# Deeper weight prefetch in the second output projection, and the first FFN matrix's second token group with contraction pairs outermost

## The chip, the cores and the metric

The kernel runs on one core of one Trainium2 chip. The metric is device time in microseconds (us) of one execution; the time of a version is the median over its runs. TensorE does matmuls and transposes (PE in the rows; PEld is its weight load), VectorE (DVE) and ScalarE (ACT) do elementwise work, GpSimd (POOL) and SyncE (SP) here mostly issue transfers.

## The reference

One step of a hybrid decoder layer in fp32, for 1024 prompt tokens and 8 sample tokens, model width 1024:

```python
mp, ... = mixer_prompt(yp * (1 + scp) + shp, w_in, sinks, gn_w, w_out)   # attention + retention, ends in [..] @ w_out
yp = layer_norm(ALPHA * yp + (1 + gtp) * mp, ln1_w, ln1_b)
g, u = split(( yp * (1 + scp2) + shp2 ) @ w_up, 2)                         # D_FF = 2816
yp = layer_norm(ALPHA * yp + (1 + gtp2) * ((silu(g) * u) @ w_down), ln2_w, ln2_b)
```

The same is done for the sample tokens. The change touches the place where the output projection (`@ w_out`) of the second half of the tokens ends, the first layer norm runs, and the first of the `w_up` matrices starts.

## The kernel before, in words

**Exactness.** Every fp32 operand of a large matmul is split into a high part (an ACT copy into a shortened format) and a low part (a DVE subtraction). A product is three matmuls, `mm3` (lines 215 to 217): high x high, high x low, low x high. So TensorE can run only when ACT and DVE have both parts of both operands.

**Output projection.** `out_proj(half, with_s)` works on 512 tokens: two column groups (`cg`) of 512 columns, four units (`kp`) of 256 contraction rows each. A unit's weights are loaded as one 512 KB tile `raw` (line 256, on SP's queue), `w_hi` makes `wh` (line 269, ACT), `w_lo` makes `wl` (line 281, DVE). `w_get` is called for each unit and runs these three ahead by the three numbers of `depth`: loads, high parts, low parts. It starts as `[2, 1, 0]`, and the second half sets it. The rows of `x` for the residual (`xr`, line 1152, and `xrs` for the samples) are loaded at the fourth unit of the first column group. In the second column group of the second half, tile 0 runs through all four units first and tiles 1 to 3 follow; `out_evac` (lines 1117, 1118) multiplies by the gate and adds the residual, and `ln1_tile` normalizes a tile (DVE statistics, a power on POOL, line 1238 on ACT). `poutz` (line 1174) is the samples' product.

**Input of the FFN.** `h2_group(g)` builds the right-hand side for token group g (512 tokens; group 1 also carries the samples, so its tiles have 260 columns instead of 256). For each of four contraction pairs j, `blocks(j)` transposes two 128-row slices through PSUM (`h2p`, line 1292) and scales them into `ht` (line 1293, ACT). Of `ht` come `hb` (split of two quarters, lines 1305 and 1306), `ts` (three differences, lines 1318 to 1320), `hs` (split of `ts` by the helper `split`, lines 1351 and 1352) and `hc` (split of one quarter, lines 1324 and 1325).

**FFN matrices.** Each matrix i is multiplied by a scheme with seven products (`STEP`, p = 1, 2, 6, 7, 5, 3, 4) instead of eight. Products 1 and 2 read `hb`, 3 reads `hc`, and 4 to 7 read `hs`. `up(i, gs)` has the product outermost, then the group, then the pair j; products that are only summed share a PSUM bank, and `up_out` evacuates them. The weights are prepared by `up_prep`: `up_load` (`wr`, line 1361), `up_sums` (lines 1370 to 1373) and the splits `wa`, `wb`, `wc` (lines 1351, 1352) and `wd` (1392, 1393), some steps ahead; for matrices after the first only once `"ahead"` is in `done`. `up_prep(-7)` and `up_prep(-3)` for the first matrix stand between the tiles of the projection's last column group.

**Order.** The generators emit work in an interleaving that `Merge` makes from the nanoseconds in each `yield`; `("need", x)` waits until x is in `done`. A main stream (`out_proj`, then `ffn`) runs with side streams (`ln1_tile`, `h2_group`, ...) at a ratio (1.73 and 1.9). The tile framework then orders each engine's instructions, with earlier emission as priority, and gives out buffers: 46 pages of 1040 columns for nearly everything in SBUF, 8 banks in PSUM. A page is given back when its last reader is done, and a load may have to wait for one.

In `ffn`, the first matrix is done for group 0, then for group 1, then all other matrices for both groups.

Of the kernel before, what the change touches and what calls it, by code (L numbers as in the profile page):

```python
# [12 lines left out]
AF = mybir.ActivationFunctionType  # L13
ALU = mybir.AluOpType
# [10 lines left out]
WID = 256, 260  # L25
# [152 lines left out]
def emit(ctx, tc, I, O):  # L178
# [10 lines left out]
    def bank(name, dt=F32):  # L189
        return psp.tile([128, 512], dt, name=name, tag="ps", bufs=8)  # L190
# [7 lines left out]
    def f(ap):  # L198
        return ap.bitcast(F32)

    M = Merge()
    done = M.done
# [925 lines left out]
    def out_proj(half, with_s):  # L1128
        yield ("need", ("att", half))
        if half == 1:  # L1130
            depth[:] = [3, 2, 1]
        for cg in range(2):
            by_tile = half == 1 and cg == 1
            ps = [bank(f"pout{t}") for t in range(4)]
# [141 lines left out]
    def h2_group(g):  # L1276


        n = WID[g]
        for t in range(4):  # L1280
            yield "need", ("xn", 4 * g + t)
        yield "need", "ab2"
        if g:
            yield "need", "xns"
        def blocks(j):
            ht = page(f"ht{g}_{j}")
            hv = ht[:, 0:4 * n].rearrange("p (s b c) -> p s b c", s=2, b=2)
            for s in range(2):
                kt = 2 * j + s
                b = bank("h2p")  # L1290
                for i in range(4):
                    PE.transpose(b[:, i * 128:(i + 1) * 128], xr[4 * g + i][:, kt * 128:(kt + 1) * 128], ident)
                A.activation(out=hv[:, s, :, 0:256], in_=b.rearrange("p (b c) -> p b c", b=2), func=AF.Identity,
                             scale=A2[:, kt, 0:1], bias=B2[:, kt, 0:1])
                if g:
                    V.tensor_copy(out=hv[:, s, :, 256:260], in_=h2ts[:, kt, :].rearrange("p (b c) -> p b c", b=2))
            return ht

        hts = []
        for j in range(4):  # L1300
            ht = blocks(j)
            hts.append(ht)
            h3 = ht[:, 0:4 * n].rearrange("p (q c) -> p q c", q=4)
            hb = page(f"hb{g}_{j}", F32R)
            A.copy(out=hb[:, 0:2 * n].rearrange("p (q c) -> p q c", q=2), in_=h3[:, 0::2, :])  # L1305
            V.tensor_sub(out=hb[:, 2 * n:4 * n].rearrange("p (q c) -> p q c", q=2), in0=h3[:, 0::2, :],  # L1306
                         in1=f(hb[:, 0:2 * n]).rearrange("p (q c) -> p q c", q=2))
            HB[g, j] = hb
            yield 880, 0, 1000
        for t in range(4 * g, 4 * g + 4):  # L1310
            x = xr.pop(t)
            G.dma_start(out=yd[t], in_=x[:, 0:1024])
        done.add(("h2b", g))
        for j in range(4):
            ht, hts[j] = hts[j], None
            h3 = ht[:, 0:4 * n].rearrange("p (q c) -> p q c", q=4)
            ts = page(f"ts{g}_{j}")
            V.tensor_sub(out=ts[:, 0:2 * n].rearrange("p (q c) -> p q c", q=2), in0=h3[:, 1::2, :], in1=h3[:, 0:2, :])
            V.tensor_sub(out=ts[:, 2 * n:3 * n], in0=h3[:, 3], in1=ts[:, 0:n])
            V.tensor_sub(out=ts[:, 3 * n:4 * n], in0=h3[:, 2], in1=ts[:, 2 * n:3 * n])  # L1320
            if j % 2 == 0:
                hc = page(f"hc{g}_{j}", F32R)
            HC[g, j], o = hc, 2 * n * (j % 2)
            A.copy(out=hc[:, o:o + n], in_=h3[:, 3])
            V.tensor_sub(out=hc[:, o + n:o + 2 * n], in0=h3[:, 3], in1=f(hc[:, o:o + n]))
            HS[g, j] = split(ts, f"hs{g}_{j}", 4 * n)
            yield 0, 0, 3400
        done.add(("h2", g))
        yield 0, 0

# [18 lines left out]
    def split(t, name, n=1024):  # L1349
        h, l = page(name + "h", F32R), page(name + "l", F32R)  # L1350
        A.copy(out=h[:, 0:n], in_=t[:, 0:n])
        V.tensor_sub(out=l[:, 0:n], in0=t[:, 0:n], in1=f(h[:, 0:n]))  # L1352
        return h, l
# [185 lines left out]
    def up(i, gs):  # L1539
        for x, p in enumerate(STEP):  # L1540
            up_prep(7 * i + x)
            for g in gs:
                c = {1: 0, 2: 0, 6: 1, 7: 1, 5: 2, 3: 2, 4: 3}[p]
                first = p in (1, 6, 5, 4)
                if first:
                    UB[i, g, c] = bank("up")
                ps = UB[i, g, c][:, 0:WID[g]]
                for j in range(4):
                    wh, wl = up_of(i, p, j)
                    hh, hl = h2_of(p, g, j)  # L1550
                    mm3(ps, wh, wl, hh, hl, j == 0 and first, j == 3, not first)
                    if j % 2:
                        yield 715
                up_out(i, g, p)
            for fn, P in side.get(7 * i + x, ()):
                fn(P)


    DSTEP = (1, 2, 6, 5, 3, 7, 4)
    ORD = [(p, k) for p in DSTEP for k in range(NP)]  # L1560
# [70 lines left out]
    def ffn():  # L1631
        yield ("need", ("h2", 0))
        yield from up(0, (0,))
        yield ("need", ("h2b", 1))
        done.add("ahead")
        for n, r in enumerate(up(0, (1,))):
            yield r
            if n == 2:
                yield ("need", ("h2", 1))
        for i in range(1, len(mats)):  # L1640
            for n, r in enumerate(up(i, (0, 1))):
                yield r
# [229 lines left out]
```

## Time and profile before

| | us |
|---|---|
| median of 3 runs | 1264.09 |
| lowest, highest | 1263.04, 1267.8 |
| the profiled execution | 1269.28 |
| its span in the profile | 1267.3 |
| TensorE busy in it | 1219.0 (96%) |
| VectorE busy | 874.9 (69%) |
| ScalarE busy | 470.8 (37%) |

Rows of an engine in order of time give start, duration, engine, line, operation, output <- inputs and shapes; in brackets stands the idle time before and what ended it. Rows by stage give the stage, its length, then busy time and instruction count of PE, PEld, DVE, ACT and POOL, the clock that was granted to TensorE (1.00 is full), the share of the DMA engines and GB/s. Matmuls overlap, so the distance from start to start is their cost and the duration is longer.

### The profile page before, as it was taken

Reading aid. Unit: us, or ns where it says so; the run is one execution under the profiler, and the core shown is the slowest. Engines: PE = TensorE matmul, PEld = TensorE weight load, DVE = VectorE, ACT = ScalarE, POOL = GpSimd, SP = SyncE. Lnnn points to the kernel's source line nnn. Section 1 sums busy time; section 2 is a strip of 40 time slices with the busy share of each in tenths; the row PEclk is TensorE's granted clock in tenths of the full one; section 3 lists DMA queues with packets and bytes.
Section 4 is the critical chain, followed back from the end, with each engine's and each line's share of the span. In section 5 each row is a group of like instructions: output and inputs, shape, how many; then the busy total and the mean of one; then the engine's idle time right before and its main releaser. Section 6 shows DMA issues by size and latency. Waiting matters only on the chain.

```text
span 1267.3 us, 20192 instructions
## 1 busy us (share of the span) xinstructions
PE 1219.0 (96%) x7923; PEld 1024.9 (81%) x7923; DVE 874.9 (69%) x1747; ACT 470.8 (37%) x876; POOL 94.7 (7%) x130
## 2 busy tenths in 40 slices
PE   8999989999999999797999999999999999999996
PEld 5877756778777677486999999999999987888885
DVE  2456665787655686876766676767676769849697
ACT  2335543355553345344233322232223234534320
POOL 0000000000000002020110111011101110000011
PEclk8999989999999999897999999999999999999998
DMA  9732487242226433312344444444434499856631
GB/s 290 225 117 68 133 266 249 69 157 83 64 67 216 150 118 107 119 69 67 128 133 157 158 142 144 131 159 142 161 115 159 142 355 393 264 160 211 201 121 67
DMA packets 143999, 198.81 MB, mean 157 GB/s; under 512 B 8127, under 2 KB 85163, under 8 KB 143888
## 3 DMA queue, kind: packets, MB, share of 16 engines
q1 hardware_dynamic: 133376, 161.11, 39.4%
q0 software_dynamic: 10528, 36.42, 7.5%
q8 instruction: 62, 1.02, 0.3%
q14 instruction: 33, 0.27, 0.1%
HBM read 154.76 MB, written 43.77 MB: 157 GB/s over the span
## 4 chain that ended last, share of the span: by engine, by line
PE 44%; issue 29%; DVE 7%; POOL 4%; DMA 1%; ACT 0%; POOLq 0%; SPq 0%; DVEq 0%
PE dn L216 4%; PE dn L215 4%; PE dn L217 4%; PE pin L215 4%; PE pin L216 4%; PE pin L217 4%; PE up L215 2%; PE up L217 2%; PE up L216 2%; PE pout L215 2%; PE pout L216 2%; PE pout L217 2%; PE adab L878 1%; POOL fd L1490 1%; DVE z L1600 1%
## 5 line engine op out<-in xcount | busy, mean ns | idle before, releaser
L215 PE MATMUL pin<-wh,hT 128*128 128x512 f32 (+1 forms) x320 | 129.6, 410 | 1.8 <-ACT qk L781 1.6
L216 PE MATMUL pin<-wl,hT 128*128 128x512 f32 (+1 forms) x320 | 125.6, 392 | 3.3 <-DVE wl L281 3.3
L217 PE MATMUL pin<-wh,hT 128*128 128x512 f32 (+1 forms) x320 | 124.6, 391 | 0.0
L215 PE MATMUL up<-hb,wa_h 128*128 128x256 f32 (+1 forms) x352 | 100.2, 285 | 2.0 <-ACT hb L1305 1.5
L216 PE MATMUL up<-hb,wa_h 128*128 128x256 f32 (+1 forms) x352 | 100.1, 284 | 0.7 <-DVE hb L1306 0.7
L217 PE MATMUL up<-hb,wa_l 128*128 128x256 f32 (+1 forms) x352 | 99.6, 283 | 0.9 <-DVE wa_l L1352 0.9
L215 PEld LDWEIGHTS pin<-wh,hT 128*128 128x128 f32 x320 | 60.9, 191 | 31.2 <-issue 13.9
L281 DVE TENSOR_TENSOR wl<-raw,wh 128x1024 fp32r<-128x1024 f32 (+1 forms) x62 | 73.1, 1183 | 8.1 <-ACT wh L269 4.4
L216 PEld LDWEIGHTS pin<-wl,hT 128*128 128x128 f32 x320 | 61.9, 193 | 14.4 <-DVE wl L281 3.4
L217 PEld LDWEIGHTS pin<-wh,hT 128*128 128x128 f32 x320 | 61.6, 193 | 14.1 <-issue 0.8
L1457 ACT ACTIVATE sg<-sg 128x256 f32<-128x256 f32 (+1 forms) x66 | 27.7, 420 | 121.8 <-DVE sg L1456 121.8
L215 PEld LDWEIGHTS up<-hb,wa_h 128*128 128x128 f32 x352 | 67.0, 190 | 2.9 <-ACT hb L1305 1.9
L216 PEld LDWEIGHTS up<-hb,wa_h 128*128 128x128 f32 x352 | 67.0, 190 | 1.3 <-DVE hb L1306 1.3
L217 PEld LDWEIGHTS up<-hb,wa_l 128*128 128x128 f32 x352 | 66.9, 190 | 1.1 <-DVE wa_l L1352 1.1
L269 ACT CAST wh<-raw 128x1024 fp32r<-128x1024 f32 (+1 forms) x62 | 62.9, 1019 | 7.0 <-DMA raw<-in_w_in 6.5
L216 PE MATMUL pout<-wl,mh 128*128 128x512 f32 x128 | 52.1, 407 | 9.8 <-DVE wl L281 9.8
L1476 ACT COPY hTs<-sg 128x8 f32<-128x8 f32 x22 | 4.3, 198 | 138.7 <-DVE sg L1463 138.7
L1456 DVE TENSOR_TENSOR sg<-up,tp 128x256 f32<-128x256 f32 (+1 forms) x66 | 27.9, 422 | 39.5 <-PE up L217 39.5
L1462 DVE TENSOR_TENSOR uc<-up,tp 128x256 f32<-128x256 f32 x66 | 28.2, 427 | 38.9 <-PE up L217 38.8
L217 PE MATMUL pout<-wh,ml 128*128 128x512 f32 x128 | 51.4, 401 | 0.0
L215 PE MATMUL pout<-wh,mh 128*128 128x512 f32 x128 | 51.2, 412 | 0.0
L216 PE MATMUL up<-hc,wc_h 128*128 128x256 f32 (+1 forms) x176 | 50.1, 285 | 0.0
(502 smaller groups left out, 3627.0 us busy)
## 6 DMA issues: line engine op xcount, KB each, us to landing
wr<-in_w_up SPq DMA_DIRECT2D x44, 512.0 KB, 5.2
raw<-in_w_in SPq DMA_DIRECT2D x38, 512.0 KB, 3.9
adr<-in_w_ada_ffn SPq DMA_DIRECT2D x24, 512.0 KB, 3.7
wd<-in_w_down SPq DMA_DIRECT2D x22, 512.0 KB, 5.2
dr<-fs SPq DMA_DIRECT2D x44, 256.0 KB, 3.5
dr<-ws SPq DMA_DIRECT2D x44, 256.0 KB, 3.1
fd<-sg POOLq DMA_DIRECT2D x33, 256.0 KB, 4.0
dr<-fd SPq DMA_DIRECT2D x33, 256.0 KB, 8.6
```

The costliest lines, as they stand in the source:

```text
L215: PE.matmul(ps, lhsT=ah, rhs=bh, start=start, stop=False, skip_group_check=onto)
L216: PE.matmul(ps, lhsT=ah, rhs=bl, start=False, stop=False, skip_group_check=onto)
L217: PE.matmul(ps, lhsT=al, rhs=bh, start=False, stop=stop, skip_group_check=onto)
L269: A.copy(out=h[:, 0:n], in_=src[:, 0:n])
L281: V.tensor_sub(out=l[:, 0:n], in0=src[:, 0:n], in1=f(h[:, 0:n]))
L878: PE.matmul(b[32 * q:32 * q + 32, :], lhsT=cT[:, k2 * 4 + q, :], rhs=rr[q // 2][:, (q % 2) * 512:(q % 2) * 512 + 512], start=k2 == 0, stop ...
L1456: V.tensor_tensor(out=dst, in0=ps, in1=add, op=ALU.add)
L1457: A.activation(out=dst, in_=dst, func=AF.Silu)
L1462: V.tensor_tensor(out=t, in0=ps, in1=add, op=ALU.add)
L1476: A.copy(out=ffs[:, (2 * P + e) % 8, 0:8].rearrange("p (b c) -> p b c", b=2), in_=t[:, 512:NT].rearrange("p (b c) -> p b c", b=2)[:, :, 25 ...
L1490: G.dma_start(out=two(d) if p == 4 else d, in_=ap)
L1600: V.tensor_tensor(out=x[0:rows, 0:1024], in0=x[0:rows, 0:1024], in1=ln1wb[j][0:rows, 0:1024], op=(ALU.mult, ALU.add)[j])
```

## The change

The depth for the second half of the output projection becomes loads 4, high parts 4 and low parts 3 units ahead.

`h2_group` (for both groups) finishes one pair at a time: `hb` high, `ts`, `hb` low, the next pair's `blocks`, then `hs` and `hc`; it reports each pair as `("h2j", g, j)`, and the stores of `yd` come after the loop. `blocks` of at most two pairs are alive.

A new function, `up_by_pair`, does the first matrix for group 1. The pair is its outermost loop: all seven products of a pair follow when that pair is reported. Each product has a PSUM bank of its own until the last pair, so seven banks are held; products 1 and 2, formerly summed in one bank, and 6 and 7, and 5 and 3, are now summed when they are evacuated. `"ahead"` is set when pair 0 of group 1 is reported.

```diff
         if half == 1:
-            depth[:] = [3, 2, 1]
+            depth[:] = [4, 4, 3]
...
-        hts = []
+        ht, hc = blocks(0), None
         for j in range(4):
-            ht = blocks(j)
-            hts.append(ht)
             h3 = ht[:, 0:4 * n].rearrange("p (q c) -> p q c", q=4)
             hb = page(f"hb{g}_{j}", F32R)
             A.copy(out=hb[:, 0:2 * n].rearrange("p (q c) -> p q c", q=2), in_=h3[:, 0::2, :])
-            V.tensor_sub(out=hb[:, 2 * n:4 * n]..., in0=h3[:, 0::2, :], in1=f(hb[:, 0:2 * n])...)
-            HB[g, j] = hb
-            yield 880, 0, 1000
-        for t in range(4 * g, 4 * g + 4):
-            x = xr.pop(t)
-            G.dma_start(out=yd[t], in_=x[:, 0:1024])
-        done.add(("h2b", g))
-        for j in range(4):
-            ht, hts[j] = hts[j], None
             ts = page(f"ts{g}_{j}")
             V.tensor_sub(out=ts[:, 0:2 * n]..., in0=h3[:, 1::2, :], in1=h3[:, 0:2, :])
             V.tensor_sub(out=ts[:, 2 * n:3 * n], in0=h3[:, 3], in1=ts[:, 0:n])
             V.tensor_sub(out=ts[:, 3 * n:4 * n], in0=h3[:, 2], in1=ts[:, 2 * n:3 * n])
+            V.tensor_sub(out=hb[:, 2 * n:4 * n]..., in0=h3[:, 0::2, :], in1=f(hb[:, 0:2 * n])...)
+            HB[g, j] = hb
+            nxt = blocks(j + 1) if j < 3 else None
+            HS[g, j] = split(ts, f"hs{g}_{j}", 4 * n)
...
-            HS[g, j] = split(ts, f"hs{g}_{j}", 4 * n)
-            yield 0, 0, 3400
+            ht = nxt
+            done.add(("h2j", g, j))
+            yield 880, 0, 3700
+        for t in range(4 * g, 4 * g + 4):
+            x = xr.pop(t)
+            G.dma_start(out=yd[t], in_=x[:, 0:1024])
...
+    def up_by_pair(i, g):
+        P, n, o = mats[i][0], WID[g], 256 * g
+        ub = {}
+        p1, u2 = TP[i][:, o:o + n], TP[i][:, 516 + o:516 + o + n]
+        for j in range(4):
+            yield ("need", ("h2j", g, j))
+            done.add("ahead")
+            for x, p in enumerate(STEP):
+                up_prep(7 * i + (7 * j + x) // 4)
+                if j == 0:
+                    ub[p] = bank("up")
+                ps = ub[p][:, 0:n]
+                wh, wl = up_of(i, p, j)
+                hh, hl = h2_of(p, g, j)
+                mm3(ps, wh, wl, hh, hl, j == 0, j == 3)
+                yield 375
+                if j < 3:
+                    continue
+                if p == 1:
+                    A.copy(out=p1, in_=ps)
+                elif p == 6:
+                    V.tensor_tensor(out=u2, in0=ps, in1=p1, op=ALU.add)
+                elif p == 7:
+                    V.tensor_tensor(out=p1, in0=ps, in1=u2, op=ALU.add)
+                else:
+                    F, b = {2: (0, 0), 5: (1, 1), 3: (0, 1), 4: (1, 0)}[p]
+                    dst = f_at(2 * P + F, g, b)
+                    V.tensor_tensor(out=dst, in0=ps, in1=u2 if p == 3 else p1, op=ALU.add)
+                    A.activation(out=dst, in_=dst, func=AF.Silu)
+                if p == 5:
+                    V.tensor_tensor(out=u2, in0=ps, in1=u2, op=ALU.add)
...
         yield from up(0, (0,))
-        yield ("need", ("h2b", 1))
-        done.add("ahead")
-        for n, r in enumerate(up(0, (1,))):
-            yield r
-            if n == 2:
-                yield ("need", ("h2", 1))
+        yield from up_by_pair(0, 1)
```

More of the change, by code (lines that the diff above doesn't have):

```diff
@@ L1305, in h2_group @@
             A.copy(out=hb[:, 0:2 * n].rearrange("p (q c) -> p q c", q=2), in_=h3[:, 0::2, :])
-            V.tensor_sub(out=hb[:, 2 * n:4 * n].rearrange("p (q c) -> p q c", q=2), in0=h3[:, 0::2, :],
-                         in1=f(hb[:, 0:2 * n]).rearrange("p (q c) -> p q c", q=2))
-            HB[g, j] = hb
-            yield 880, 0, 1000
-        for t in range(4 * g, 4 * g + 4):
-            x = xr.pop(t)
-            G.dma_start(out=yd[t], in_=x[:, 0:1024])
-        done.add(("h2b", g))
-        for j in range(4):
-            ht, hts[j] = hts[j], None
-            h3 = ht[:, 0:4 * n].rearrange("p (q c) -> p q c", q=4)
             ts = page(f"ts{g}_{j}")
@@ L1320, in h2_group @@
             V.tensor_sub(out=ts[:, 3 * n:4 * n], in0=h3[:, 2], in1=ts[:, 2 * n:3 * n])
+            V.tensor_sub(out=hb[:, 2 * n:4 * n].rearrange("p (q c) -> p q c", q=2), in0=h3[:, 0::2, :],
+                         in1=f(hb[:, 0:2 * n]).rearrange("p (q c) -> p q c", q=2))
+            HB[g, j] = hb
+            nxt = blocks(j + 1) if j < 3 else None
+            HS[g, j] = split(ts, f"hs{g}_{j}", 4 * n)
             if j % 2 == 0:
```

## The prediction

> **What bounds the kernel now.** I read the page first: TensorE (PE) is busy 96% of the span, so the time can only fall where PE stands still or runs at a low clock.
>
> ```profile
> span 1267.3 us, 20192 instructions
> PE 1219.0 (96%) x7923; PEld 1024.9 (81%) x7923; DVE 874.9 (69%) x1747; ACT 470.8 (37%) x876; POOL 94.7 (7%) x130
> PE   8999989999999999797999999999999999999996
> ```
>
> Beside a dip at slice 10, two stand in the PE line at slices 17 and 19 (31.7 us each), where the diff's code runs. Next I cut that stretch by stage (us; busy time and instruction count of PE, weight loads, DVE, ACT, POOL; granted clock; DMA share, GB/s):
>
> ```profile
> 498.60:510.00 11.40, 11.40 (x69) 8.38 (x68) 3.14 (x5) 10.73 (x16) 1.93 (x4) 1.00 0.88 321
> 510.00:521.10 11.10, 11.10 (x51) 6.42 (x49) 10.14 (x18) 4.35 (x7) 0.00 (x0) 1.00 0.41 147
> 521.10:530.70 9.60, 1.05 (x6) 0.48 (x3) 9.43 (x16) 1.99 (x2) 0.00 (x0) 0.75 0.38 109
> 530.70:557.00 26.30, 26.29 (x101) 18.67 (x102) 21.74 (x37) 7.94 (x8) 2.32 (x3) 0.90 0.05 21
> 557.00:566.40 9.40, 8.00 (x62) 7.25 (x60) 6.09 (x17) 7.18 (x9) 4.82 (x7) 1.00 0.32 130
> 566.40:577.00 10.60, 8.38 (x65) 7.24 (x64) 5.53 (x18) 8.61 (x14) 0.13 (x1) 1.00 0.46 138
> 577.00:592.00 15.00, 10.12 (x52) 9.20 (x51) 10.52 (x20) 6.57 (x11) 0.00 (x0) 0.73 0.00 1
> 592.00:601.40 9.40, 7.95 (x43) 7.45 (x44) 7.44 (x11) 2.77 (x5) 0.00 (x0) 0.70 0.39 113
> 601.40:621.20 19.80, 19.80 (x168) 19.76 (x168) 13.90 (x27) 4.93 (x9) 1.12 (x2) 1.00 0.22 67
> ```
>
> Hole one is 521.1 to 530.7, with PE at 1 of 9.6 us and DVE full: the second output projection. Hole two is 557 to 601.4: the first FFN matrix, with every engine partly idle and the clock near 0.7 at the end. From 601.4 PE is steady: 168 matmuls in 19.80 us, 0.118 us each.
>
> **Part one: projection weights further ahead.** PE and DVE in order of time (start, duration, idle before and what ended it), and two rows of ACT:
>
> ```profile
> 530.71 0.80 PE L216 MATMUL pout<-wl,mh 128*128 128x512 f32 x1 [8.56 <-DVE wl L281]
> ...
> 533.57 1.92 PE L1174 MATMUL poutz<-raw,mixTs 128*32 128x512 f32 x4
> ...
> 536.34 0.39 PE L215 MATMUL pout<-wh,mh 128*128 128x512 f32 x1
> 536.57 0.39 PE L216 MATMUL pout<-wl,mh 128*128 128x512 f32 x1
> ...
> 503.54 0.69 DVE L1306 TENSOR_TENSOR hb<-ht,hb 128x512 fp32r<-128x512 f32 x1 [4.95 <-ACT hb L1305]
> ...
> 513.49 1.22 DVE L281 TENSOR_TENSOR wl<-raw,wh 128x1024 fp32r<-128x1024 f32 x1
> ...
> 529.45 1.21 DVE L281 TENSOR_TENSOR wl<-raw,wh 128x1024 fp32r<-128x1024 f32 x1
> ...
> 535.38 3.49 DVE L281 TENSOR_TENSOR wl<-raw,wh 128x1024 fp32r<-128x1024 f32 x3
> ...
> 512.22 1.04 ACT L269 CAST wh<-raw 128x1024 fp32r<-128x1024 f32 x1
> ...
> 496.22 4.64 ACT L1238 ACTIVATE xr<-xr,lrs 128x1024 f32<-128x1024 f32 x4 [8.96 <-DVE lrs L1236]
> ```
>
> The first unit of the second column group had its high part at 512.22, but DVE made the low part only at 529.45: seventeen microseconds late in DVE's own order, not for want of data. PE loses 8.56 us waiting. It then runs slowly from 530.71 to 536.34: in those 5.63 us stand eight 512-column matmuls, which take 0.23 us each afterwards (536.34 to 536.57), and the four narrow ones of 533.57, which I put at half of their 1.92 us. That is 2.8 us of work, so another 2.8 us is lost. Ceiling of part one: 8.56 + 2.8 = 11.4 us.
>
> Nothing is removed: five low parts (1.2 us each on DVE) and their high parts (1.04 on ACT) are issued earlier. DVE has 4.95 us idle before 503.54 and is busy 3.14 of 11.4 us up to 510; ACT has 8.96 idle before 496.22. Three low parts fit there, 3.6 us taken from the full stretch behind. The new order inside `h2_group(0)` helps as well: the differences and `hs` splits of a pair can go between its `hb` pieces in 503 to 510, where DVE waited for ACT; up to 5 us of it moves forward. What is late next is DVE: between 530.7 and 557 it is busy 21.74 of 26.3, and if PE takes 11.4 less there, there are 26.3 - 2.8 = 23.5 us for 21.7 - 2.4 (two low parts gone ahead) plus a backlog carried in from hole one, 9.4 us less the two low parts (2.4) and less the 5 moved ahead: 2 us. That makes 21.3 of 23.5, 91%. DVE is not that dense anywhere in these rows but in 510 to 530.7 (19.57 of 20.7), and a stage in which each piece waits for PE or ACT in turn seldom is; so I take not the 11.4 but 8.
>
> The loads move too. One more 512 KB weight load now goes ahead of the four `xr` loads and `xrs` in SP's queue, and those wait for pages today:
>
> ```profile
> SPq L1152 <- PE pout L216: 18.8, 1, 18.8
> 504.11 1.98 SPq L1152 DMA_DIRECT2D xr<-in_x  x4
> ```
>
> So pages are short here, and each piece kept ahead takes one of 46 (about five more); against that, `h2_group` now keeps two `ht` pages alive where it kept four. `xr` is first needed when the first column group is evacuated, near 521, 17 us after 504.11: that slack is the cover; without it the evacuation and PE's next banks slip by what is missing. Ends for part one: 0 (the stall only moves to DVE or pages) and 11.4.
>
> **Part two: pairs outermost.** DVE, ACT and PE for the second token group; the last three rows are groups (ns shortest/median/longest):
>
> ```profile
> 569.16 0.63 ACT L1305 CAST hb<-ht 128x520 fp32r<-128x520 f32 x1
> ...
> 575.84 0.70 DVE L1306 TENSOR_TENSOR hb<-ht,hb 128x520 fp32r<-128x520 f32 x1 [0.70 <-ACT hb L1305]
> 576.45 0.42 DVE L1319 TENSOR_TENSOR ts<-ht,ts 128x260 f32<-128x260 f32 x1
> 576.79 0.42 DVE L1325 TENSOR_TENSOR hc<-ht,hc 128x260 fp32r<-128x260 f32 x1
> ...
> 578.68 1.24 DVE L1352 TENSOR_TENSOR hs_0l<-ts,hs_0h 128x1040 fp32r<-128x1040 f32 x1 [0.79 <-ACT hs_0h L1351]
> 579.84 0.69 DVE L1318 TENSOR_TENSOR ts<-ht 128x520 f32<-128x520 f32 x1
> ...
> 592.23 1.24 DVE L1352 TENSOR_TENSOR hs_3l<-ts,hs_3h 128x1040 fp32r<-128x1040 f32 x1 [1.18 <-ACT hs_3h L1351]
> 593.39 0.68 DVE L1370 TENSOR_TENSOR sb<-wr 128x512 f32<-128x512 f32 x1
> ...
> 577.56 0.58 PE L215 MATMUL up<-hb,wa_h 128*128 128x260 f32 x1 [0.47 <-ACT tp L1438]
> 577.94 0.42 PE L216 MATMUL up<-hb,wa_h 128*128 128x260 f32 x1
> 578.15 0.42 PE L217 MATMUL up<-hb,wa_l 128*128 128x260 f32 x1
> ...
> 599.45 0.39 PE L217 MATMUL up<-hb,wa_l 128*128 128x256 f32 x1 [0.94 <-DVE wa_l L1352]
> ...
> L1293 ACT ACTIVATE ht<-h2p,B,A x16: 761/772/779, 501.4 to 574.4; 128x512 f32<-128x512 f32 x16
> L1296 DVE COPY ht<-h2ts x8: 164/165/171, 568.1 to 572.5; 128x8 f32<-128x8 f32 x8
> L1351 ACT CAST hs_0h<-ts x2: 1050/1054/1059, 511.3 to 577.6; 128x1024 fp32r<-128x1024 f32 x1, 128x1040 fp32r<-128x1040 f32 x1
> ```
>
> The chain today: four `hb` first, then pair by pair `ts`, `hs`; the last `hs_3l` starts at 592.23; then come the next matrix's four sums (from 593.39) and its `wa_l`, for which PE waits until 599.45. The order by products does not let PE finish early, because every one of the `hs` products needs all four pairs.
>
> With the change, DVE's floor per pair is, start to start: `hb` 0.61 (575.84 to 576.45), three 260-column pieces of 0.34 (576.45 to 576.79), `hs` 1.16 (578.68 to 579.84), the first `ts` 0.6 like `hb`, two small copies 0.2: 3.6 us. ACT's, by durations, is two `ht` 1.54, `hb` 0.63, `hs` 1.05 and `hc` some 0.4 (as long as DVE's): at most 3.6 us, less start to start. So DVE bounds it: 4 x 3.6 = 14.5 us from about 569.2, plus three evacuations of the first group (1 us), gives 584.7 for the last pair. Then sums (4 x 0.6) and `wa_l` (1.2, as `wl`) of the next matrix: 588.3, against 599.4 now. PE has 21 matmuls per pair, 2.5 us at 0.118, within the 3.6; after the last low part some 11 remain, 1.3 us. That is 11.1 us at best. Today each `hs` costs DVE 0.7 to 1.2 us of waiting for ACT (0.79 and 1.18 above), and those handoffs will not all be filled: I take 2 us off, so 9. The other end is 0: the next matrix's weights stay as late as now.
>
> Small edits, together: the product sums formerly made in PSUM cost two more DVE additions (0.34 each), hidden behind 601.4 to 621.2 where DVE is busy 13.9 of 19.8; PE's matmul count is unchanged. The four `yd` stores on POOL move behind the loop; POOL is idle there (0.00 in 577 to 592), so they cost nothing unless they are issued so late that their pages hold back the next `wr` loads. Those loads, `ahead`, come no later in SP's queue; SP has nothing else then. The seven banks are treated below.
>
> The clock: from 577.94 a matmul takes 0.21 us start to start, not 0.118, after a wait of 0.47 us; 577 to 592 was granted 0.73, although PE stood still only in short pieces. So I count the half-speed stretches in both versions alike, at no difference. [...]
>
> **Sum.** 8 + 9 = 17 us. The profiled execution took 1269.28 us (span 1267.3, 2.0 around it), 5.2 above the median of 1264.09. So 1252 in its terms and 1264.1 - 17 = 1247 for the median. DVE has room: over 498.6 to 601.4 the eight rows add up to 74.0 busy of 102.8 us, and 17 takes 59% of the 28.8 left. That is 86% occupancy, dense but below the 98% of hole one.
>
> **Rivals.** *Only one half pays.* If part one's gain is eaten by DVE order or by pages (the 18.8 us wait speaks for it), 1264.1 - 9 = 1255; if part two's is eaten by late weights of the next matrix, 1256. Against it: both stalls name work that is ready but late in order.
>
> *The change does not do what it says.* DVE is full wherever PE waits in hole one, and the same DVE work merely meets PE a stage later; 1 to 3 us remain: 1262. For it: 9.43 of 9.6. Against: the idle 4.95, and DVE under 80% busy in every stage of hole two.
>
> *Slower: one PSUM bank for the transposes.* `up_by_pair` holds seven of eight banks from its first pair to its last, and the transposes of later pairs need two per pair. If they are ordered behind the products, the pairs run one after another: transposes 0.93 (32 in 3.71 us today), `ht` 1.5, `ts` 1.28, `hs` 1.06 + 1.24, products 2.5 = 8.5 us per pair. Four from 567 end at 601, so part two gains nothing, and above that it loses. PE would then be mostly idle and at half clock: 3.4 more per pair, 614.6, 13 to 14 us later, less 8 of part one: 1270. It outweighs part one's 8 us above 10.5 us a pair. Against it today:
>
> ```profile
> 566.99 3.71 PE L1292 MATMUL h2p<-cst,xr 128*128 128x128 f32 x32
> ```
>
> All 32 ran in one block before any product of this group.
>
> **How the numbers follow.** 0.5% (6.3 us) is about what a measurement of this kernel can tell from no change. Both parts pay: 0.62, 1247, its own range 1239 to 1254. One part pays: 0.20, near 1255.5, of which 0.05 lies within 0.5%. Little happens: 0.10, 1262. One bank: 0.08, 1270, a tenth of it within. So faster 0.77, same 0.15, slower 0.08. The low end is both ceilings (11.4 + 11.1 = 22.5) and the clock that the last stage lost (9.4 us at 0.70, 2.8): 1264.1 - 25.3 = 1239; the high end takes in the little-happens case: 1263.
>
> **What would show it.** Part one: no wait of PE on `wl` above 2 us, `wl` rows of the last group before about 515, the last `pout` near 549 instead of 556.75. Part two: `hs` low parts of the second group 3.6 to 4.2 us apart with the last near 585 less part one's shift, products of all four weight groups inside each pair, next `wa_l` about 10 us earlier relative to the last `pout`. I am wrong if PE waits on DVE in the projection for as long as before, if `xr` loads land after the first column group ends, if `h2p` transposes come in separate blocks between products with `ht` waiting for them, or if the next matrix's `wa_l` is what PE waits for by more than 3 us.

## The result, and the profile after

Six runs of the changed kernel have a median of 1257.87 us (1254.73 to 1261.39); six of the kernel before 1265.76 (1263.04 to 1269.35). The ratio is 0.9936, 95% interval 0.9912 to 0.9959: 8 us or 0.64% faster. The forecast was 17 us. The profiled execution took 1258.56 us, 0.7 above its median, where that of before was 3.5 above its own; so of the 10.5 us between the two spans only some 8 are the change.

The page of the changed kernel, its span, busy times and TensorE in 40 slices:

```profile
span 1256.8 us, 20184 instructions
PE 1213.2 (97%) x7923; PEld 1023.8 (81%) x7923; DVE 875.0 (70%) x1749; ACT 469.6 (37%) x876; POOL 93.9 (7%) x130
PE   8999989999999999987999999999999999999996
```

The dip at slice 17 is gone (9 for 7); that at slices 18 and 19 is still there (8 and 7; before 9 and 7). The same stretch by stage, cut as in the prediction up to 601.4:

```profile
498.60:510.00 11.40, 11.40 (x68) 8.47 (x67) 4.11 (x9) 9.17 (x14) 2.54 (x5) 1.00 0.47 185
510.00:521.10 11.10, 11.10 (x58) 7.26 (x56) 9.89 (x17) 6.91 (x12) 0.00 (x0) 1.00 0.83 285
521.10:530.70 9.60, 9.60 (x41) 6.99 (x42) 9.46 (x16) 2.39 (x4) 0.00 (x0) 1.00 0.20 58
530.70:557.00 26.30, 18.96 (x99) 15.07 (x98) 24.45 (x50) 10.14 (x12) 5.28 (x8) 0.98 0.15 60
557.00:566.40 9.40, 9.17 (x74) 8.81 (x73) 4.20 (x13) 6.78 (x10) 1.09 (x2) 0.89 0.17 62
566.40:577.00 10.60, 8.89 (x42) 7.90 (x43) 8.69 (x20) 7.08 (x13) 0.00 (x0) 0.68 0.37 99
577.00:592.00 15.00, 10.49 (x66) 9.41 (x65) 11.53 (x21) 5.89 (x11) 0.00 (x0) 0.81 0.26 72
592.00:601.40 9.40, 9.40 (x76) 9.40 (x76) 7.70 (x12) 4.22 (x6) 0.00 (x0) 0.93 0.39 107
```

Hole one is closed: 521.1 to 530.7 holds 9.60 us of PE where it held 1.05. DVE is no emptier for it (9.46), and fuller in the next stage: 24.45 of 26.3 us where it was 21.74. In that stage PE is now busy for only 18.96 us, where it was 26.29. The hole has moved to the right, and the clock from 557 to 592 is 0.68 to 0.89. TensorE in order of time shows what it waits for; the row without brackets is the block of transposes for the second group:

```profile
533.88 0.50 PE L216 MATMUL pout<-wl,mh 128*128 128x512 f32 x1 [1.23 <-DVE wl L281]
545.76 0.39 PE L215 MATMUL up<-hs_0h,wb_h 128*128 128x256 f32 x1 [1.19 <-ACT wb_h L1347]
550.55 0.38 PE L215 MATMUL up<-hb,wa_h 128*128 128x256 f32 x1 [3.12 <-ACT tp L1434]
...
555.44 0.38 PE L217 MATMUL up<-hs_0h,wc_l 128*128 128x256 f32 x1 [1.80 <-DVE wc_l L1348]
560.34 3.71 PE L1292 MATMUL h2p<-cst,xr 128*128 128x128 f32 x32
587.40 0.58 PE L215 MATMUL up<-hb,wa_h 128*128 128x256 f32 x1 [3.26 <-ACT wa_h L1347]
```

The 8.56 us on `wl` became 1.23 (its last low parts begin at 532.62, below), and the last projection matmul comes at 543.9 instead of 556.7. But then the first matrix's first group takes from 544 to 560, where it took 9.4 us (556.98 to 566.40): waits of 1.19 (`wb_h`), 3.12 (`tp`) and 1.80 us (`wc_l`). The transposes start at 560.34 against 566.99: of some 13 us, 6.65 are left. (Of both, 1.4 us lies before this stretch, where the two profiled executions already differ: the next section compares them from a mark that is the same in both. The change itself moved the projection's end by 11.4 us and the transposes by 5.2.)

DVE, first and second group, the weights' low parts, and the next matrix's `wa_l` (lines 1347 and 1348 are now the `split` helper, 1305 to 1307 `ts`, 1452 an evacuation of the first group's products):

```profile
504.97 0.69 DVE L1305 TENSOR_TENSOR ts<-ht 128x512 f32<-128x512 f32 x1 [5.21 <-ACT ht L1293]
508.22 1.23 DVE L1348 TENSOR_TENSOR hs_0l<-ts,hs_0h 128x1024 fp32r<-128x1024 f32 x1 [1.11 <-ACT hs_0h L1347]
525.74 1.21 DVE L1348 TENSOR_TENSOR hs_3l<-ts,hs_3h 128x1024 fp32r<-128x1024 f32 x1
532.62 2.34 DVE L281 TENSOR_TENSOR wl<-raw,wh 128x1024 fp32r<-128x1024 f32 x2
...
565.83 1.24 DVE L1348 TENSOR_TENSOR hs_0l<-ts,hs_0h 128x1040 fp32r<-128x1040 f32 x1 [1.13 <-ACT hs_0h L1347]
570.58 1.24 DVE L1348 TENSOR_TENSOR hs_1l<-ts,hs_1h 128x1040 fp32r<-128x1040 f32 x1 [0.78 <-ACT hs_1h L1347]
574.99 1.24 DVE L1348 TENSOR_TENSOR hs_2l<-ts,hs_2h 128x1040 fp32r<-128x1040 f32 x1 [1.13 <-ACT hs_2h L1347]
579.23 0.42 DVE L1452 TENSOR_TENSOR sg<-up,tp 128x256 f32<-128x256 f32 x1 [0.42 <-PE up L217]
581.63 1.23 DVE L1348 TENSOR_TENSOR hs_3l<-ts,hs_3h 128x1040 fp32r<-128x1040 f32 x1
588.41 1.22 DVE L1348 TENSOR_TENSOR wa_l<-wr,wa_h 128x1024 fp32r<-128x1024 f32 x1
```

ACT around the two longest of those waits and at the end of the normalization:

```profile
549.00 1.24 ACT L1238 ACTIVATE xr<-xr,lrs 128x1024 f32<-128x1024 f32 x1 [3.30 <-DVE lrs L1236]
550.15 0.35 ACT L1434 COPY tp<-up 128x256 f32<-128x256 f32 x1
557.47 1.23 ACT L1238 ACTIVATE xrs<-xrs,lrs 8x1024 f32<-8x1024 f32 x1
585.66 0.76 ACT L1583 ACTIVATE sg<-sg 128x260 f32<-128x260 f32 x2 [0.25 <-DVE sg L1582]
586.32 1.03 ACT L1347 CAST wa_h<-wr 128x1024 fp32r<-128x1024 f32 x1
```

Three things stand in these rows. The copy of product 1 (`tp`, 550.15) stands behind a normalization in ACT's order that began at 549.00, because its statistics came late from DVE; PE's 3.12 us hang on that. PE's transposes follow without a pause on the first group's products, which the waits above made late, and on the samples' transposes (559.75), whose rows (`xrs`, from 557.47) are normalized at 558.70. In both groups DVE waits for ACT's high part (1.11 us before 508.22); in the second it stands 1.13, 0.78 and 1.13 us before the first three `hs` low parts until ACT has made the high part; the four low parts are 4.75, 4.41 and 6.64 us apart. And `wa_h` of the next matrix (586.32) stands behind all silus of the second group in ACT's order, so PE waits 3.26 us for it and then runs slowly (0.58 us for that matmul, 0.38 for its like at 550.55). Its data were not what was late: the two loads were issued at 567.1 and 567.6, and loads of this kind land 4.4 to 6.5 us after their issue.

### The profile page after: what moved, and what is told of

Its sections match the earlier page's. It is cut to its first block, busy times and chain, and to the rows that moved or that the text cites. A ratio compares the mean times of both kernels' runs of the same rounds, so it can differ in the third digit from the quotient of the medians.

```text
span 1256.8 us, 20184 instructions
## 1 busy us (share of the span) xinstructions
PE 1213.2 (97%) x7923; PEld 1023.8 (81%) x7923; DVE 875.0 (70%) x1749; ACT 469.6 (37%) x876; POOL 93.9 (7%) x130
## 4 chain that ended last, share of the span: by engine, by line
PE 54%; issue 29%; DVE 9%; POOL 4%; DMA 2%; ACT 1%; POOLq 0%; SPq 0%; DVEq 0%
PE pin L215 6%; PE pin L216 6%; PE pin L217 6%; PE dn L216 4%; PE dn L217 4%; PE dn L215 4%; PE up L215 2%; PE up L217 2%; PE up L216 2%; PE adab L878 2%; PE pout L215 1%; POOL fd L1486 1%; PE pv L671 1%; PE sps L628 1%; PE pout L216 1%
## 5 line engine op out<-in xcount | busy, mean ns | idle before, releaser
L215 PEld LDWEIGHTS pin<-wh,hT 128*128 128x128 f32 x320 | 61.1, 192 | 31.0 <-issue 13.9
```

The lines of the kernel that those rows point to most:

```text
L215: PE.matmul(ps, lhsT=ah, rhs=bh, start=start, stop=False, skip_group_check=onto)
```

## The experiments

All positions below are relative to the first transpose of the first group (T0), read from rows as these two (instances, ns shortest/median/longest, first and last start), changed kernel: T0 499.8, last projection matmul 543.9 - 499.8 = 44.1, last transpose of the second group 563.8 - 499.8 = 64.0.

```profile
L217 PE MATMUL pout<-wh,ml x128: 387/395/482, 413.5 to 543.9; 128*128 128x512 f32 x128
...
L1292 PE MATMUL h2p<-cst,xr x64: 270/273/332, 499.8 to 563.8; 128*128 128x128 f32 x64
```

Each position is from one execution; times are medians, and ratios are to runs of the kernel before on the same chip.

The prefetch moves T0 itself. The projection's operations ahead of the first transpose, in the kernel before and in the changed one (stretch, length, then busy time and count of PE, PEld and DVE, clock, DMA share, GB/s):

```profile
0.00:498.58 498.58, 57.50 (x228) 41.56 (x228) 5.30 (x8) 0.97 0.46 146
0.00:499.77 499.77, 60.01 (x239) 43.61 (x239) 5.21 (x8) 0.98 0.46 147
```

With the prefetch, 239 projection matmuls stand ahead of the first transpose instead of 228, in every kernel that has it. Eleven more of them are 2.6 us: from a matmul some 100 us earlier, which all kernels share, T0 is 105.8 us away before and 108.4 in the changed kernel (in executions that lose 1.6 us less on the way 104.2 without the prefetch and 106.8 with it). So wherever a kernel with the prefetch is set against one without, 2.6 us has to be added to its positions; such a position is called shifted below. The expectations give unshifted ones.

**The first four: who takes the projection's gain?** Theory A: DVE is the bound until the first layer norm is done, so PE's earlier projection is handed back. B: both gains are independent, as predicted. C: TensorE's own stretch and ACT's order set the second group's start.

*The prefetch alone*, in the kernel before:

```diff
-            depth[:] = [3, 2, 1]
+            depth[:] = [4, 4, 3]
```

> The kernel before with the depth 4, 4, 3 alone. Theory A (the projection's gain is handed back because VectorE is the bound up to the end of the first layer norm): the last projection matmul comes 11 us earlier than before, the second group's transposes only 6 to 7 us earlier, and the span falls by 5 to 6 us. Theory B (the two gains are independent, as the prediction had it): the span falls by 8 to 11 us.

1266.28 us (12 runs), ratio 1.001 [0.9992, 1.0028]: nothing. The projection ends at +47.4 and the transposes at +69.2. Shifted, these are +50.0 instead of +58.1, 8.1 us earlier, and +71.8 instead of +71.8: the second group starts no earlier at all. Its waits, and the last `hs` low part of the first group:

```profile
533.93 0.50 PE L216 MATMUL pout<-wl,mh 128*128 128x512 f32 x1 [2.34 <-DVE wl L281]
549.95 0.58 PE L217 MATMUL up<-hb,wa_l 128*128 128x256 f32 x1 [4.25 <-DVE wa_l L1352]
...
537.94 1.21 DVE L1352 TENSOR_TENSOR hs_3l<-ts,hs_3h 128x1024 fp32r<-128x1024 f32 x1
```

With the old order of the first group, that last low part comes at +42.8 shifted (before +35.6, changed kernel +28.5 shifted): the early `wl` pushed the splits back, and PE waits 2.34 on `wl` and 4.25 on `wa_l`. B, which gave the prefetch alone 8 us, is out; the 5 to 6 us that A left of it did not come either.

*Both new orders without the prefetch*, the changed kernel with `depth[:] = [3, 2, 1]`:

> The changed kernel with the depth back at 3, 2, 1: pairs outermost alone. Theory A: the wait of 8 us in the projection is there again, the stretch from the second group's first ht to its last hs low part is 21 to 23 us where it was 25.8 before, and the span falls by 3 to 5 us. Theory B: it falls by 9 us.

1261.66 us (12 runs), ratio 0.9968 [0.995, 0.9985], some 4 us. Alone, the prefetch gives nothing; added to the new orders it gives 4 by the medians, though the intervals with it and without it (0.9912 to 0.9959) just overlap.

*Less work on DVE*, the changed kernel with the six additions of the samples' projection left out and one ACT copy in their place:

```diff
-        samp_sum(tmp[0:8], psz, 512)
+        A.copy(out=tmp[0:8], in_=psz[0:8, 0:512])
```

> The changed kernel without the six VectorE additions that sum the samples' four partial projections (those rows of the result then hold one partial sum): some 3.6 us less VectorE work between 519 and 538 us. Theory A (VectorE is the bound there): the second group's transposes start 2 to 3.6 us earlier than in the changed kernel and the span falls by as much. Theory C (TensorE's own stretch, its waits for ScalarE and its low clock, sets that start): the transposes move by under 1 us and the span stays within 1 us.

1255.91 us (6 runs), ratio 0.9927 [0.9903, 0.9952]. The projection ends where it did (+43.8), the transposes at +61.1 instead of +64.0, the last `hs` low part at +78.6 instead of +81.8. The additions take 0.68 us each on DVE in the changed kernel, 4.1 in all, and without them the second group comes 3 us earlier, as A has it. The time alone (2 us) would not have told it.

*Products 1 and 2 in banks of their own*, as a test of C:

```diff
-                first = p in (1, 6, 5, 4)
+                first = p in (1, 6, 5, 4) or (i == 0 and p == 2)
```

> The changed kernel with products 1 and 2 of the first matrix's first group in PSUM banks of their own, so that TensorE need not wait until ScalarE has copied product 1 (a wait of 3.1 us in the changed kernel, behind a layer norm in ScalarE's order). Theory C: the wait goes and the second group's transposes start 2 to 3 us earlier, the span falls by 2 to 3 us. Theory A: the wait goes, but the rows that are transposed are normalized no earlier (the last at 558.6 us), so the transposes come at most 1 us earlier and the span stays within 1 us.

1258.38 us, ratio 0.9942 [0.9922, 0.9963], transposes at +63.8. The 3.12 us wait on `tp` is gone, and this one has taken its place:

```profile
548.61 0.46 PE L217 MATMUL up<-hs_0h,wb_l 128*128 128x256 f32 x1 [2.61 <-DVE wb_l L1348]
```

So PE's longest wait was not the bound: the next DVE piece comes 2.61 us too late as well. C, as far as it rests on that wait, is out.

**Which part needs which.** The new order sits in `h2_group`, which serves both groups, so the change has three parts: prefetch (P), first group's order (0), second group's order with `up_by_pair` (1). Four kernels fill the table.

> Both new orders are in one function, which also serves the first token group. This kernel has the deeper prefetch (4, 4, 3) and the new order of the first group's splits (ht, hb, ts, next pair's transposes, hs, hc), but the second group is prepared and multiplied as before (all transposes, then all differences; column outermost). Theory D (the two edits need each other: the deeper prefetch only moves the projection if VectorE has its first-group splits behind it, and the new order of the first group lets it do them in 503 to 511 instead of 520 to 535): relative to the first group's first transposes the last pout matmul comes at about +44 and the second group's transposes at about +64 as in the changed kernel, and the time is 3 to 6 us below before, since only the second group's own part is missing. Rival (the gain of the pair comes from the second group's order): last pout and transposes as with the deeper prefetch alone (+47, +69), time as before within 2 us.

> The changed kernel with the first token group's splits in the old order (all transposes and hb first, then the differences); the prefetch (4, 4, 3) and the second group's pairs outermost stay. Theory D (the first group's order pays for the prefetch): transposes of the second group no earlier than +67 to +69 relative to the first ones, where the changed kernel has +64; time 1260 to 1263, half of the gain or more is gone. Rival (the second group's order is what counts): time as the changed kernel, 1257 to 1259, transposes at +64.

> Only the first token group's splits in the new order; prefetch (3, 2, 1) and the second group as before. Theory D (prefetch and first group's order need each other): by itself it gives little, 0 to 3 us less than before, since the projection still waits about 8 us for wl; together with the prefetch they gave 5.8. Rival (the first group's order is a gain by itself, and the prefetch adds nothing to it): 1258 to 1259, as with both.

> Only the second token group prepared and multiplied pair by pair; prefetch (3, 2, 1) and the first group's order as before. With this run every combination of the three parts (prefetch, first group's order, second group's order) has a time. Theory: what this part saves is the second group's own stretch, first transposes to last hs low part, about 3 us of it, and 1 to 3 us of time; rival (prediction's part two): 8 to 9 us.

Last projection matmul, last transpose of the second group, and last `hs` low part are relative to T0; "own stretch" is the distance between the last two. In the rows with P the positions are shifted, that is 2.6 us larger than in their traces. The us column is the ratio's distance from 1 times 1264.

| parts | ratio, interval | us | projection | transposes | last hs | own stretch |
|---|---|---|---|---|---|---|
| none | 1 | 0 | 58.1 | 71.8 | 93.6 | 21.8 |
| P | 1.0010 [0.9992, 1.0028] | +1.3 | 50.0 | 71.8 | 92.6 | 20.8 |
| 0 | 0.9989 [0.9973, 1.0006] | -1.4 | 57.2 | 69.7 | 90.6 | 20.9 |
| 1 | 1.0007 [0.9990, 1.0025] | +0.9 | 57.9 | 71.6 | 89.0 | 17.4 |
| P, 0 | 0.9954 [0.9939, 0.9970] | -5.8 | 46.8 | 65.6 | 86.5 | 20.9 |
| P, 1 | 0.9994 [0.9978, 1.0009] | -0.8 | 50.0 | 70.9 | 88.5 | 17.6 |
| 0, 1 | 0.9968 [0.9950, 0.9985] | -4.0 | 57.3 | 69.8 | 87.3 | 17.5 |
| P, 0, 1 | 0.9936 [0.9912, 0.9959] | -8.1 | 46.7 | 66.6 | 84.4 | 17.8 |

By the times, no part alone makes a difference that can be told from nothing; their three effects add up to +0.8 us, and all together give -8.1. Prefetch and first group's order need each other (+1.3 and -1.4 alone, -5.8 together), and the transposes say the same: the prefetch moves them by 0.0 and 0.7 us with the old order of the first group (the time by +1.3 and -1.7), and by 4.1 and 3.2 us with the new one (the time by -4.4 and -4.1). The second group's own stretch shrinks by 3 to 4.4 us where part 1 is added; by the medians 2.1 to 2.6 us of that reach the end, except where it stands alone, but none of these differences is by itself clear of the intervals.

**The two waits that the change left.** *Differences one pair ahead*, so that DVE makes `ts` of pair j+1 while ACT copies `hs` of pair j (both groups, same instructions):

```diff
             nxt = blocks(j + 1) if j < 3 else None
+            nts = diffs(nxt, j + 1) if j < 3 else None
             HS[g, j] = split(ts, f"hs{g}_{j}", 4 * n)
```

> The changed kernel with the differences ts of a pair computed one pair ahead, so that VectorE works on ts of pair j+1 while ScalarE copies hs_h of pair j (the same instructions in another order, in both groups). Theory (hand-offs between VectorE and ScalarE stretch the second group's pairs from 3.6 to 4.4-6.6 us): the waits of 0.8 to 1.1 us for hs_h are gone, hs low parts stand 3.6 to 4.2 us apart but for the last, the last one comes 2 to 3 us earlier relative to the first transposes (+79 instead of +82), the time 0 to 3 us below the changed kernel's. Rival (the next matrix's weights wa1 bound the end of this stage): hs earlier, the first product of the next matrix not, time unchanged.

1252.85 us (4 runs), ratio 0.9909 [0.9885, 0.9933]. DVE's low parts of the second group, and PE's first product of the next matrix:

```profile
560.55 1.23 DVE L1354 TENSOR_TENSOR hs_0l<-ts,hs_0h 128x1040 fp32r<-128x1040 f32 x1
564.29 1.24 DVE L1354 TENSOR_TENSOR hs_1l<-ts,hs_1h 128x1040 fp32r<-128x1040 f32 x1
567.82 1.24 DVE L1354 TENSOR_TENSOR hs_2l<-ts,hs_2h 128x1040 fp32r<-128x1040 f32 x1
571.50 1.24 DVE L1354 TENSOR_TENSOR hs_3l<-ts,hs_3h 128x1040 fp32r<-128x1040 f32 x1 [0.16 <-ACT hs_3h L1353]
...
578.04 0.58 PE L215 MATMUL up<-hb,wa_h 128*128 128x256 f32 x1 [2.71 <-ACT wa_h L1353]
```

Spacing is 3.74, 3.53 and 3.68 us, the own stretch 13.3 instead of 17.8, and the last low part comes at +75.8 instead of +81.8: 6 us, more than the 2 to 3 expected. The wait on `wa_h` stays (2.71 us), as the rival said, so the end moved by less than that. The interval overlaps the changed kernel's.

*Next matrix's loads earlier*, which puts `wa_h` ahead of three silus in ACT's order:

```diff
         yield ("need", ("h2", 0))
+        for r in [r for r in prep_list if r[1] == 1 and r[3] is up_load]:
+            prep_list.remove(r)
+            up_load(1)
         yield from up(0, (0,))
```

> The changed kernel with the two loads of the next matrix's weights (wr1) issued ahead of the first group's products, which also moves the copy wa1_h ahead of three of the second group's silus in ScalarE's order. Theory: TensorE's wait of 3.26 us for wa1_h at 587.4 falls to under 1 us and the half clock behind it is shorter, 2 to 4 us less time. Rival (the last silus and their VectorE additions then end later, and the next matrix's second weight group is late instead): time within 1 us of the changed kernel.

1254.67 us (4 runs), ratio 0.9924 [0.9895, 0.9953]; the wait on `wa_h` is gone, one of 1.24 on `wb_h` follows. Its interval too overlaps the changed kernel's, so alone this is not shown by the time to gain.

*Both:*

> The changed kernel with both of the last two edits: the differences ts one pair ahead, and the next matrix's weight loads ahead of the first group's products. Theory (two different waits, VectorE's for hs_h and TensorE's for wa1_h): the wait of 2.7 us for wa1_h goes, 1249 to 1252, below either alone (1252.9 and 1254.7). Rival (they remove the same slack): 1253 as with the first alone.

1244.12 us (4 runs, 1242.97 to 1246.89), ratio 0.9849 [0.9827, 0.9872]: 19 us below before, faster than both kernels of the comparison, and below the 1249 to 1252 expected. From 560 to 620 PE waits at most 0.86 us for anything. In order of time, `wa_h` on ACT and PE's longest wait at the start of the next matrix; then two stages by the windows:

```profile
572.11 1.04 ACT L1353 CAST wa_h<-wr 128x1024 fp32r<-128x1024 f32 x1
...
574.84 0.39 PE L215 MATMUL up<-hs_0h,wb_h 128*128 128x256 f32 x1 [0.84 <-ACT wb_h L1353]
```

```profile
560.00:575.00 15.00, 12.48 (x93) 11.44 (x94) 14.60 (x29) 10.58 (x18) 0.00 (x0) 1.00 0.14 39
575.00:590.00 15.00, 15.00 (x127) 14.96 (x128) 13.67 (x26) 5.04 (x9) 0.00 (x0) 1.00 0.37 103
```

`wa_h` comes at 572.11 instead of 586.32, before the second group's silus, and the clock is 1.00 where the changed kernel had 0.68 and 0.81. By the ratios the two edits are worth 11 us together, and 1.5 (the loads) and 3.4 (the differences) apart: each alone left the other's wait in the way. That they give more together than the sum is not clear of the intervals. In the traces the 336th matmul on the `up` weights, two matrices' worth, comes 4.4 us earlier after T0 than in the changed kernel with the loads, 4.9 with the differences and 11.3 with both, so there most of the 11 is the sum.

**The predicted terms, measured where nothing blocks them.** From this kernel each of the two predicted terms was taken away: the prefetch, and the second group's order.

> The kernel of both edits (differences a pair ahead, next weights early; 1244.1) with the prefetch back at 3, 2, 1. It measures what the prediction's part one is worth once the path behind the projection is free of the other waits. If the predicted 8 us was right for a free path: 1251 to 1253 (ratio to before about 0.990 to 0.992). If the prefetch is worth only what it was worth in the changed kernel as measured (1261.7 without it, 1257.9 with it): 1247 to 1249.

> The kernel of both edits with the second token group prepared and multiplied as before (all transposes, then all differences; column outermost). It measures what the prediction's part two is worth once its hand-offs and the wait for the next weights are gone. If the predicted 9 us was right for a free path: 1252 to 1254 (ratio about 0.991). If it is worth the 2 us that it is worth in the changed kernel: 1246 to 1247.

Without the prefetch 1249.02 us, ratio 0.9883 [0.9863, 0.9903]: by the medians the prefetch is worth 4 to 5 us, though the two intervals just overlap. Projection and transposes, first with it, then without:

```profile
L217 PE MATMUL pout<-wh,ml x128: 387/394/483, 408.7 to 537.8; 128*128 128x512 f32 x128
L1292 PE MATMUL h2p<-cst,xr x64: 270/273/330, 494.9 to 556.3; 128*128 128x128 f32 x64
```

```profile
L217 PE MATMUL pout<-wh,ml x128: 387/393/628, 410.0 to 547.5; 128*128 128x512 f32 x128
L1292 PE MATMUL h2p<-cst,xr x64: 270/273/329, 493.6 to 560.2; 128*128 128x128 f32 x64
```

The projection ends at +45.5 shifted or +53.9, 8.4 us apart; the last transpose stands at +64.0 shifted or +66.6, 2.6 apart; the time is 4.9 apart. Without the second group's order 1257.16 us, ratio 0.9943 [0.9924, 0.9963], the last `hs` low part at +82.2 instead of +74.8: 12 to 13 us. The edit puts the whole old order back for this group, so it also takes out the differences one pair ahead there; the 12 to 13 us are the worth of both, not of part two as predicted.

**Two subtractions on GpSimd.** In the kernel of both edits DVE is busy 28.9 of the 30 us from 500 to 530 and GpSimd not at all, so the low parts of the first group's pairs 2 and 3 were moved to GpSimd:

```diff
-            HS[g, j] = split(ts, f"hs{g}_{j}", 4 * n)
+            HS[g, j] = split(ts, f"hs{g}_{j}", 4 * n, G if g == 0 and j > 1 else None)
```

> The kernel of both edits with two 128x1024 subtractions of the first group (hs low parts of pairs 2 and 3, 1.2 us each on VectorE) moved to GpSimd, which the trace shows idle between 498 and 536. Theory (VectorE is the bound from 500 to the end of the first layer norm): projection's end or second group's transposes 1 to 2.4 us earlier relative to the first transposes, time 0 to 2 us below the kernel of both edits. Rival (GpSimd is several times slower or holds VectorE up while it runs): no gain or a loss of some us; the trace shows it as longer VectorE instructions beside the GpSimd ones.

1245.99 us, ratio 0.9861 [0.9838, 0.9884], against 0.9849: no gain, and the second group's last transpose stands at +63.4 instead of +61.4. GpSimd's two rows, and DVE beside them; then the same two DVE operations without GpSimd:

```profile
513.94 2.98 POOL L1354 TENSOR_TENSOR hs_2l<-ts,hs_2h 128x1024 fp32r<-128x1024 f32 x1 [16.43 <-ACT hs_2h L1353]
518.37 2.44 POOL L1354 TENSOR_TENSOR hs_3l<-ts,hs_3h 128x1024 fp32r<-128x1024 f32 x1 [1.44 <-ACT hs_3h L1353]
...
514.28 0.41 DVE L1303 TENSOR_TENSOR ts<-ht,ts 128x256 f32<-128x256 f32 x1
515.33 1.88 DVE L1304 TENSOR_TENSOR ts<-ht,ts 128x256 f32<-128x256 f32 x1
519.23 2.11 DVE L1124 TENSOR_TENSOR otz<-otz,gates 8x512 f32<-8x512 f32 x1
```

```profile
515.66 0.41 DVE L1304 TENSOR_TENSOR ts<-ht,ts 128x256 f32<-128x256 f32 x1
519.94 0.68 DVE L1124 TENSOR_TENSOR otz<-otz,gates 8x512 f32<-8x512 f32 x1
```

GpSimd took 2.98 and 2.44 us for what DVE does in 1.21, and the DVE operations running at its end take 1.88 and 2.11 instead of 0.41 and 0.68: 2.9 us longer for 2.4 taken off. Not every DVE operation beside GpSimd is longer: the `ts` at 514.28 lies inside the recorded GpSimd span as well and took its usual 0.41. What decides which one is, and how exact that span is, no run here shows.

## Why the prediction was wrong

**The step that failed is the size of part two's term.** In the prediction's own terms, part one is the prefetch together with the first group's new order, of which it counted in 5 us of DVE work. That kernel (row P, 0) is 5.8 us faster, 3.8 to 7.7 by its interval, where 8 was forecast. Part two on top of it makes 8.1: 2.3 us by the medians, at most 7.3 by the ends of the two intervals, where 9 was forecast. Adding the two terms was not the fault, for together they give no less than apart (part one alone 5.8 us faster, part two alone 0.9 slower). What the sum hid lies inside part one: by the times, of prefetch and order neither pays without the other.

**Part one.** In the five pairs of kernels that differ in the prefetch alone the projection's end moved by 7.9 to 10.6 us: somewhat less than the ceiling of 11.4. What was wrong is how much of it passes on. I wrote that DVE would be 91% dense up to 557; it was 93% dense (24.45 of 26.3), and of the prefetch's 10.6 us in the changed kernel 3.2 came through to the transposes and 4 to the time (last two rows of the table). At that density the layer norm's statistics, the weight sums and the splits that the second group needs are all behind each other on DVE, and PE's earlier end only finds the same queue; 4.1 us of additions taken off DVE there brought the second group 3 us forward. A free path did not help much: 2.6 us to the transposes there, 4.9 to the time. The 5 us that I let move ahead of 510 were also too many: DVE's busy time in 498.6 to 510 rose from 3.14 to 4.11, because it waits 5.21 us for the first `ht` in this version too (504.97), and the prefetch puts eleven more matmuls ahead of the transposes that `ht` needs. What did move is the order behind it: the last `hs` low part of the first group came 7.1 us earlier (+28.5 shifted, before +35.6), and by the table this, which I had as a help in one sentence, is what the prefetch lives on.

**Part two.** Two things were priced too low or not at all. I took 2 us off for handoffs; they cost 0.8 to 1.1 a pair, and the last pair also stood behind an evacuation that waits for PE (579.23), so the first to last low part took 15.8 us where the same instructions take 10.95 with the differences one pair ahead. And I priced the next matrix by DVE's `wa_l`, whose signpost failed: 588.41 is 44.5 us after the last projection matmul, before it was 41.4, not ten earlier. What PE waited for was `wa_h` on ACT, an engine that I had counted as having room. It has; its order puts `wa_h` last. With both waits removed the kernel gains another 11 us, and DVE's spacing is then 3.5 to 3.7 us, the floor of 3.6 that I worked out. So the floor was right, and what it takes to reach it was not in the change. On that kernel part two and the differences one pair ahead together are worth 12 to 13 us, above my best case of 11.1.

**Signposts.** Right: no wait of PE on `wl` above 2 us; all 32 transposes in one block, so the bank rival did not come; the last projection matmul at 543.9, even earlier than the 549 named. Wrong: the last column group's `wl` rows (two of the four only from 532.62, not before about 515), `hs` spacing, last `hs`, `wa_l`. Wrong too: the products of all four weight groups inside each pair. PE did the `wd` products of pairs 0 to 2 only from 579.75 to 580.78, behind the first group's last products (577.61 to 578.91); no run shows why. And the `xr` loads, issued at 510.91 instead of 504.11, landed as late as 519.2, after the first column group's last matmul (515.7), which I had named as a sign of being wrong; the first addition that needs them starts at 526.87 with no idle time of DVE before it, so no wait in the trace goes back to them.

**The clock.** I counted half-speed stretches alike in both. In the changed kernel the clock is 0.68 from 566.40 to 577, where no wait of PE is above 0.6 us; with both waits removed it is 1.00 from 560 to 590. Within these stages neither the length of the waits (up to 0.6 us in the first, up to 0.86 in the second) nor the idle share tells them apart: PE is busy 8.89 us of 10.6 at 0.68, and 12.48 of 15 in the best kernel's 560 to 575 at 1.00. What sets the clock here stays open. Part of every term above is this clock, and I cannot separate it from the waits.

**Rivals.** "Only one half pays" gave 1255 to 1256, nearest to the result, and the case that it named for part two, late weights of the next matrix, is one of the two waits found. It had them late on DVE's side and the first half at its full 8 us; neither is what the runs show.

**Open.** Part 1 alone shortens its own stretch by as much as elsewhere and gains nothing by the time (+0.9, interval -1.3 to +3.2); one wait of 3.3 us on `wa_h` is there as well, but no run of it without that wait was made. The traces do not settle it: the 336th matmul on the `up` weights comes 118.5 us after T0 there, against 121.6 before, and 120.6 (shifted) with the prefetch alone, 118.1 with the first group's order alone, 113.4 (shifted) with all three. By these the three effects nearly add up. But each is one execution, and that of before was 3.5 us above its median, so whether a part alone gains nothing or 1 to 3 us stays open. T0 lies between 493.1 and 499.8 us; 2.6 of that is the prefetch, the rest differs from one execution to the next before the stretch of this change begins.

## What to carry to other kernels

A wait removed on one engine is worth what the engine it waited for can pass on: here VectorE was 93% dense behind the hole, and 3.2 of the prefetch's 10.6 us came through. In such a place take work or idle time out of VectorE's order first, then prefetch. Take positions from a mark that the change cannot move; here the prefetch moved the first transpose by 2.6 us. Forecast edits to one chain together, as an order per engine with the next late piece named, for every engine that feeds the chain; an engine that is mostly idle (ScalarE here, 37% busy) can still have the one needed copy at the end of its order, and TensorE waited 3.26 us for it. When an edit gains less than its hole was worth, look for what became late next before undoing it: here two small moves turned 8 us into 19.

## What the hardware showed that I had not expected

GpSimd is no free helper for VectorE here: two 128x1024 subtractions on it stretched single VectorE operations from 0.41 to 1.88 and from 0.68 to 2.11 us. And TensorE's clock fell to 0.68 in a stage whose single waits were all below 0.6 us (566.40 to 577), and was 1.00 there (560 to 590) once the two waits were gone.
